# A decay multiply shared by read-out and update, a gate affine folded into activations, and late conditioning blocks spread over three tiles

## The chip, the cores and the metric

The kernel runs on all 8 cores of one Trainium2 chip. Each core computes its own share of the batch; no core waits for another. The metric is the time on the device, in microseconds (us), of the slowest of the eight cores.

Executions of one kernel mostly agree within 0.3%. Some fall into a slower state, more than 1.5% above the fastest run. Ratios here compare fast runs with fast runs; medians take in all runs.

## The reference, cut to what matters

One layer of a decoder trunk: a conditioned normalisation, one input projection, a recurrence over chunks of 64 tokens, a short convolution, an output projection, and then a squared-ReLU MLP. One core has 8 prompt tiles of 256 tokens and one sample tile of 128 tokens.

```python
mod = jax.nn.silu(c) @ w_ada + b_ada                  # conditioning: w_ada is 12 blocks of 512 columns
sh1, sc1, g1, sh2, sc2, g2 = jnp.split(mod[:, None, :], N_MOD, axis=-1)
h = rms_norm(x) * (1 + sc1) + sh1                     # needs blocks 0 to 3
q, fz, i, g, gb, gc, hv = jnp.split(h @ w_in, SPLITS, axis=-1)
logf = jnp.log(lb_h + (1.0 - lb_h) * jax.nn.sigmoid(fz32))      # the gate
k = (1.0 - lb_h) * jax.nn.sigmoid(-fz32)
...
def step(s, inp):                                     # the recurrence over chunks
    d, u = inp
    return d[..., None] * s + u, s                    # the read-out uses s as well
...
x = x + g1 * mix                                      # needs blocks 4 and 5
h2 = rms_norm(x) * (1 + sc2) + sh2                    # needs blocks 6 to 9: "late"
x = x + g2 * (jnp.square(jax.nn.relu(h2 @ w_up)) @ w_down)      # needs blocks 10 and 11: "late"
```

## The kernel before: the parts that matter

A Python list scheduler fixes the order of instructions on each engine when the program is built, from a cost model. At run time each engine goes through its list in that order and waits on semaphores. It knows dependences by buffer *name*, and by overlap of address ranges. A name that covers too much gives a false dependence; a shared address gives a real one.

Weights are fp32 in memory and bf16 on the core; this kernel loads them by casting DMAs that GpSimd issues, at most six under way at a time: each waits for the sixth before it in the program's order. The same GpSimd queue does element-wise work, such as adding the mixer's result to the rows of x.

Loop over tiles, with the loads placed by hand (`n_` counts tiles from 0; tile 3 is the sample tile):

```python
    for n_ in range(2, len(tiles)):
        t0op = len(P.ops)
        if n_ + 1 < len(tiles):
            hs[n_ + 1] = norm1(*tiles[n_ + 1])
        for step in gen(n_):
            if step == "B" and n_ + 1 == len(tiles):
                WB = View(wall[2:6])
                for j in UPORD[:7]:
                    load_up(j)
                norm2(bgroups[0])
        mark = [o for o in P.ops[t0op:] if o.eng == "pe"][20:21]
        if n_ == 4:                                   # four late conditioning blocks behind one tile
            for i, j in enumerate((6, 7, 8, 9)):
                load_ada(j)
                mod_block(j, i % 2 == 0, 24 + 8 * (i // 2), 16 + 8 * (i // 2))
        if n_ == 5:
            load_ada(10); load_ada(11)
            gates(1)
        if 5 <= n_ and conv_i < 4:                    # w_down blocks, fp32 to bf16, memory to memory
            convert(CONV[conv_i], mark)
            conv_i += 1
        if n_ == 6:
            load_dn(0); load_dn(1)
```

Buffers that play a part, and who shares them:

```python
    adaR = Ring("ada", 2, [128, 8, 512], BF16, offset=u0)              # two conditioning blocks
    SbF = (one("rout", [128, 512], F32, offset=u0 + 16384), "rout")    # the last state, to be stored
    ...  # wdn[2], the third w_down block, is placed at u0 + 16384 too
    xrR = Ring("xr", 3, [128, 1024])                                   # rows of x, and the gates' tile
    mix_slot(2, at["p"])
    gfin_b = one("gfin_b", [128, 1024])                                # overlaps the third mix buffer
    modT = one("modT", [128, 32, 17])                                  # all conditioning values, one name
```

A conditioning block ends in a write of `modT`; every normalisation reads `modT`, so a late block's write and the next tile's `hT` are ordered, though they touch different columns:

```python
        tt("dve", modT[:, out_j0:out_j0 + 8, :], ..., ALU.add, [bn, "vecT"], ["modT"])          # in mod_block
        ts("dve", h[:, jj, :], Mb[...], modT[:, 8 + jj, 0:1], modT[:, jj, 0:1], ..., [Mn, "modT"], [hn])   # in norm1
```

The gate, and the recurrence for one chunk:

```python
            act(A_[:], A_[:], AF.Exp, [an], [an], scale=-1.0)
            for i, hd in enumerate(heads):
                ts("dve", F_[...], A_[...], oml[:, hd:hd + 1], lbv[:, hd:hd + 1], ALU.mult, ALU.add, ...)
            act(A_[:], F_[:], AF.Ln, [fn_], [an])
            ...
                        Sb, sbn = SbR.take()
                        tt("pool", v3(Sb), v3(Tp), bdec(dp, cp), ALU.mult, [tpn, dpn], [sbn])   # for the read-out
                        inter(ci, Sb, sbn)
                        for hd in range(4):                                                     # for the update
                            stt(Tn_[...], Tp[...], dp[:, hd, cp:cp + 1], U[...], ALU.mult, ALU.subtract, ...)
```

Of the kernel before, what the change touches and what calls it, by code (L numbers as in the profile page):

```python
# [297 lines left out]
def build_program():  # L298
# [171 lines left out]
        mix.append(t)  # L470

    mix_slot(0); mix_slot(1)
    TsR = Ring("Ts", 2, [128, 512])
    SbR = Ring("Sb", 2, [128, 512], BF16)
    smR = Ring("sm", 2, [128, 512], BF16)
    sqR = Ring("sq", 2, [128, 512], BF16)
# [1 line left out]
    ucar = one("ucar", [128, 4, 32]); uco = one("uco", [128, 4, 32])  # L478
    ucR = Ring("uc", 2, [128, 4, 2])
    decR = Ring("dec", 2, [128, 4, 4]); decS = Ring("decs", 1, [128, 4, 16])  # L480
    lbv = one("lbv", [128, 4]); oml = one("oml", [128, 4])
    vecT = one("vecT", [128, 72]); scT = one("scT", [128, 8, 17], BF16)
    at["p"] = max(at["p"], a0 + 7 * 8192)
    ada0R = Ring("adaf", 4, [128, 8, 512], BF16, offset=k0)
# [106 lines left out]
    tr([(Mb[:, j * 32:j * 32 + 17], ctb[0:17, j * 128:(j + 1) * 128], cB[0:17, 0:17]) for j in range(8)], [ctb_n, "cB"], [Mn])  # L591
    copy("act", scT[:], Mb[:, 0:256].rearrange("p (a b) -> p a b", b=32)[:, :, 0:17], [Mn], ["scT"])
    tt("dve", lbv[:], lbT[:, 1, :], lbT[:, 0, :], ALU.subtract, ["vecT"], ["lbv"])
    act(lbv[:], lbv[:], AF.Exp, ["lbv"], ["lbv"])
    act(lbv[:], lbv[:], AF.Ln, ["lbv"], ["lbv"], bias=1.0)
    act(lbv[:], lbv[:], AF.Exp, ["lbv"], ["lbv"], scale=-1.0)
    ts("dve", oml[:], lbv[:], -1.0, 1.0, ALU.mult, ALU.add, ["lbv"], ["oml"])
    ts("dve", gon, gon, math.sqrt(128.0), None, ALU.mult, None, ["vecT"], ["vecT"])

# [102 lines left out]
    def mixer_tile(kind, ti, last, h, hn, xblk):  # L702
# [12 lines left out]

        for g, heads in enumerate(groups):
            bank, bn = proj(h, hn, 1, heads, TT)
            A_, an = ER.take(); F_, fn_ = WF.take(); C_, cn = WF.take()
            act(A_[:], bank[:, :], AF.Exp, [bn], [an], scale=-1.0)
            act(A_[:], A_[:], AF.Ln, [an], [an], bias=1.0)  # L720
            act(A_[:], A_[:], AF.Exp, [an], [an], scale=-1.0)
            for i, hd in enumerate(heads):
                ts("dve", F_[:, i * TT:(i + 1) * TT], A_[:, i * TT:(i + 1) * TT], oml[:, hd:hd + 1], lbv[:, hd:hd + 1], ALU.mult, ALU.add,
                   [an, "oml", "lbv"], [fn_], mode=1.0)
            act(A_[:], F_[:], AF.Ln, [fn_], [an])
            scan(C_[:], smask, A_[:], ["cBm", an], [cn])
            act(A_[:], C_[:], AF.Exp, [cn], [an])
            act(C_[:], C_[:], AF.Exp, [cn], [cn], scale=-1.0)
            k_, kn = nkR.take()
            stt(k_[:], F_[:], 1.0, C_[:], ALU.subtract, ALU.mult, [fn_, cn], [kn])  # L730
            nk[g] = (k_, kn)
            Eg[g] = (A_, an)
            ev = A_[:].rearrange("p (h c t) -> p h c t", h=NH, t=C)
            copy("pool", dec[:, heads[0]:heads[0] + NH, 0:NCH], ev[:, :, :, C - 1], [an], [dec_n])
        yield "F"

        vt = []
# [43 lines left out]
        for b in range(NB):  # L781
            t0 = b * 128
            v_, vn = vt[b]
            M, Mn = MR.take()
            Mb = M[:, :].bitcast(BF16)
            tr([(Mb[:, hd * 128:(hd + 1) * 128], hv(nk, hd, t0, t0 + 128), ident) for hd in range(4)], dn(nk) + ["cB"], [Mn])
            k_, kn = ktR.take()
            copy("act", k_[:], Mb[:, 0:512], [Mn], [kn])
            M, Mn = MR.take()
            mm([(M[:, hd * 128:(hd + 1) * 128], hv(nk, hd, t0, t0 + 128), hv(qd, hd, t0, t0 + 128), True, True) for hd in range(4)],  # L790
               dn(nk) + dn(qd), [Mn])
            sm, smn = smR.take()
            tt("dve", sm[:].rearrange("p (h t) -> p h t", t=128), M[:, :].rearrange("p (h t) -> p h t", t=128),
               nmask.unsqueeze(1).to_broadcast([128, 4, 128]), ALU.mult, [Mn, "cBm"], [smn])
            O, On = OR.take()
            mm([(O[:, hd * 128:(hd + 1) * 128], v_[:, hd * 128:(hd + 1) * 128], sm[:, hd * 128:(hd + 1) * 128], hd == 0, False) for hd in range(4)],
               [vn, smn], [On])

            def inter(ci, sb, sbn):
                mm([(O[:, hd * 128 + ci * C:hd * 128 + (ci + 1) * C], sb[:, hd * 128:(hd + 1) * 128],  # L800
                     hv(qd, hd, t0 + ci * C, t0 + (ci + 1) * C), False, ci == NCB - 1) for hd in range(4)], [sbn] + dn(qd), [On])

            def bdec(dt_, c):
                return dt_[:, :, c:c + 1].to_broadcast([128, 4, 128])

            v3 = lambda t: t[:].rearrange("p (h v) -> p h v", v=128)
            if kind == "p":
                for ci in range(NCB):
                    c = b * NCB + ci
                    U, Un = UR.take()  # L810
                    mm([(U[:, hd * 128:(hd + 1) * 128], k_[64 * ci:64 * ci + 64, hd * 128:(hd + 1) * 128],
                         v_[64 * ci:64 * ci + 64, hd * 128:(hd + 1) * 128], True, True) for hd in range(4)], [kn, vn], [Un])
                    Tn_, tnn = TsR.take()
                    if state["T"] is None:
                        ts("dve", Tn_[:], U[:, :], -1.0, None, ALU.mult, None, [Un], [tnn], mode=1.0)
                    else:
                        Tp, tpn, dp, dpn, cp = state["T"]
                        Sb, sbn = SbR.take()
                        tt("pool", v3(Sb), v3(Tp), bdec(dp, cp), ALU.mult, [tpn, dpn], [sbn])
                        inter(ci, Sb, sbn)  # L820
                        for hd in range(4):
                            stt(Tn_[:, hd * 128:(hd + 1) * 128], Tp[:, hd * 128:(hd + 1) * 128], dp[:, hd, cp:cp + 1],
                                U[:, hd * 128:(hd + 1) * 128], ALU.mult, ALU.subtract, [tpn, dpn, Un], [tnn])
                    state["T"] = (Tn_, tnn, dec, dec_n, c)
            else:
                for ci in range(NCB):
                    S, Sn = SlR.take()
                    dma("sp", S[:], srec_d[ci], [], [Sn], 262144)
                    Sb, sbn = SbR.take()
                    copy("act", Sb[:], S[:], [Sn], [sbn])  # L830
                    inter(ci, Sb, sbn)
                    km, kmn = kmR.take()
                    ts("dve", km[:], k_[:], cF[:, CR8 + ci:CR8 + ci + 1], None, ALU.mult, None, [kn, "cF"], [kmn], mode=1.0)
                    U, Un = UR.take()
                    mm([(U[:, hd * 128:(hd + 1) * 128], km[:, hd * 128:(hd + 1) * 128], v_[:, hd * 128:(hd + 1) * 128], True, True)
                        for hd in range(4)], [kmn, vn], [Un])
                    tt("dve", S[:], S[:], U[:, :], ALU.subtract, [Sn, Un], [Sn])
                    tt("pool", v3(S), v3(S), bdec(dec, ci), ALU.mult, [Sn, dec_n], [Sn])
                    dma("sp", recs_d[ci], S[:], [Sn], ["recs%d" % ci], 262144)


            sq, sqn = sqR.take()
            act(sq[:], O[:, :], AF.Square, [On], [sqn])
            M, Mn = MR.take()
            mm([(M[:, :], onesb, sq[:], True, True)], [sqn, "cB"], [Mn])
            R_, rn = WT.take()
            act(R_[:], M[:, :], AF.Ln, [Mn], [rn], bias=128.0 * EPS)
            act(R_[:], R_[:], AF.Exp, [rn], [rn], scale=-0.5)
            tt("dve", R_[:], O[:, :], R_[:], ALU.mult, [On, rn], [rn])
            for g, heads in enumerate(groups):  # L850
                h0 = heads[0]
                tt("pool", mx[:, h0:h0 + NH, t0:t0 + 128], R_[:, h0 * 128:(h0 + NH) * 128].rearrange("p (h t) -> p h t", t=128),
                   sg[g][0][:].rearrange("p (h t) -> p h t", t=TT)[:, :, t0:t0 + 128], ALU.mult, [rn, sg[g][1]], [mxn[hd] for hd in heads])
# [191 lines left out]
# [8 lines that stand above are left out]
                    load_up(j)  # L1053
                norm2(bgroups[0])
        mark = [o for o in P.ops[t0op:] if o.eng == "pe"][20:21]
        if n_ == 4:
            for i, j in enumerate((6, 7, 8, 9)):
                load_ada(j)
                mod_block(j, i % 2 == 0, 24 + 8 * (i // 2), 16 + 8 * (i // 2))
        if n_ == 5:  # L1060
            load_ada(10); load_ada(11)
            gates(1)
        if 5 <= n_ and conv_i < 4:
            convert(CONV[conv_i], mark)
            conv_i += 1
        if n_ == 6:
            load_dn(0); load_dn(1)
    load_up(7)
    load_gates(1)
    dma("sp", gfin_b[:], gfin_d.partition_broadcast(128), [], ["gfin_b"], 128 * 4096)  # L1070
# [67 lines left out]
```

## Time and profile before

984.65 us (median of 3 runs, 983.99 to 1009.44). The profiled core has a span of 985.7 us.

| stretch | what runs | what is seen |
|---|---|---|
| 0 to 301 us | loading, tiles 0 to 4, projections of tile 5 | mixed |
| 301 to 357 us | late conditioning blocks 6 to 9 | TensorE busy 23.7 of 56 us |
| 357 to 496 us | last three tiles (6 to 8), about 37 us each, and the last recurrence | TensorE mostly busy |
| 496 to 538.6 us | MLP, first group, up stage | TensorE busy |
| 538.6 us to the end | MLP from the first use of w_down | TensorE busy, DMA share 0.17 from 546 us on |

First the windows view of the kernel before. After the window and its length come the busy times of TensorE, its weight loads, VectorE, ScalarE and GpSimd, each with its number of instructions; then TensorE's granted clock, the share of time that the 16 DMA engines were busy, and GB/s.

```profile
301.00:326.00 25.00, 14.93 (x128) 7.35 (x127) 12.14 (x25) 4.91 (x9) 9.73 (x14) 0.73 0.37 85
326.00:357.00 31.00, 8.80 (x131) 6.09 (x128) 9.07 (x27) 5.17 (x12) 8.14 (x11) 0.57 0.95 148
0.00:301.00 301.00, 210.65 (x1940) 156.42 (x1940) 164.16 (x326) 126.61 (x249) 79.33 (x118) 0.96 0.62 145
301.00:397.00 96.00, 63.72 (x558) 41.31 (x556) 48.27 (x103) 29.96 (x61) 31.55 (x40) 0.77 0.74 146
397.00:538.60 141.60, 126.62 (x964) 84.68 (x963) 91.43 (x186) 61.99 (x126) 46.16 (x58) 0.95 0.90 170
```

In the second line TensorE is busy 8.8 of 31 us.

The chain of waits of the kernel before (start, length, what):

```profile
327.60 21.52 DMA ada_111<-w_ada
...
349.25 1.02 PE U L333 x32
```

TensorE's timeline, then VectorE's, of the kernel before (start, length, instruction; in brackets the idle time before it and what ended it):

```profile
339.21 1.00 PE L333 MATMUL U<-scT,ada_110 128*128 128x17 bf16 x32 [2.66 <-DMA ada_110<-w_ada]
349.25 1.00 PE L333 MATMUL U<-scT,ada_111 128*128 128x17 bf16 x32 [9.04 <-DMA ada_111<-w_ada]
```

```profile
350.36 0.30 DVE L367 TENSOR_TENSOR modT<-U,vecT 128x136 f32<-128x136 f32 x1 [14.54 <-PE U L333]
...
351.11 0.93 DVE L373 TENSOR_SCALAR hT_61<-M,modT 128x256 bf16<-128x256 bf16 x2
```

Blocks 8 and 9 can load only when 6 and 7 have left the two buffers, and the second of them takes 21.5 us to land. The next tile's `hT_61`, whose first transposes were done at 250 us, comes right after the `modT` write: the projections that could fill the gap wait on a name.

GpSimd's timeline of the kernel before, near the MLP's start:

```profile
531.34 0.57 POOL L394 DMA_DIRECT2D wdn_128<-w_down  x1 [32.70 <-DMA recp<-rout]
```

This is a w_down load that waits 32.7 us for the store of the last state, because it will overwrite that state's address. Nothing urgent stands behind it, so the wait is free.

Two groups of the recurrence in the kernel before (busy time, mean ns), of several alike:

```profile
L367 POOL TENSOR_TENSOR Sb_86<-Ts_84,dec_99 128x512 bf16<-128x512 f32 x8 | 8.7, 1085 | 12.4 <-DVE Ts_84 L377 12.4
L377 DVE SCALAR_TENSOR_TENSOR Ts_85<-Ts_84,dec_99,U 128x128 f32<-128x128 f32 x32 | 11.0, 344 | 3.6 <-DVE Ts_84 L377 1.8
```

### The profile page before, as it was taken

How to read it: one execution, taken by the hardware profiler on the slowest of the kernel's cores; microseconds unless marked ns; L12 is line 12 of the kernel's file. 1: busy time of each engine (PE TensorE's matmuls, PEld its weight loads, DVE VectorE, ACT ScalarE, POOL GpSimd, SP SyncE). 2: the span in 40 equal slices, each digit the busy share in tenths (PEclk: the TensorE clock that was granted, in tenths of full speed). 3: DMA queues.
4: the chain of work that ended last, by engine and by line, in shares of the span. 5: the costliest groups of instructions: out<-in, count | busy, mean ns of one | idle time of the engine just before them, and what ended most of it. 6: DMA issues, size and time to landing. Idle time of an engine off the chain costs nothing.

```text
span 985.7 us, 16852 instructions; the slowest of 8 cores (974.9 to 985.7 us)
## 1 busy us (share of the span) xinstructions
PE 836.5 (85%) x5929; PEld 519.7 (53%) x5929; DVE 477.4 (48%) x948; ACT 336.8 (34%) x711; POOL 202.1 (21%) x249
## 2 busy tenths in 40 slices
PE   0168888788775469999599999999999999999995
PEld 0147755466553247677355456545545654654762
DVE  1156566487735256966844334614443451451321
ACT  3056362256522044644334123313312330421321
POOL 1000134442234324345320110010021012001101
PEclk9999999799987769999799999999999999999998
DMA  8999760427133797859999821131022002101101
GB/s 162 206 189 186 163 181 23 150 100 226 68 92 87 145 169 171 172 144 167 172 192 180 258 88 68 45 107 43 22 86 86 1 23 85 44 2 43 64 2 43
DMA packets 27245, 109.75 MB, mean 111 GB/s; under 512 B 3781, under 2 KB 4165, under 8 KB 22298
## 3 DMA queue, kind: packets, MB, share of 16 engines
q0 software_dynamic: 5232, 39.19, 24.7%
q1 hardware_dynamic: 17034, 51.65, 16.3%
q10 hardware_dynamic: 4896, 17.83, 5.9%
q8 instruction: 48, 0.79, 0.3%
q14 instruction: 35, 0.29, 0.1%
HBM read 125.36 MB, written 26.69 MB: 154 GB/s over the span
## 4 chain that ended last, share of the span: by engine, by line
PE 64%; DMA 12%; DVE 10%; issue 7%; ACT 4%; POOL 1%; DVEq 0%; ACTq 0%; POOLq 0%
PE G L333 34%; PE U L333 21%; PE O L333 8%; DMA win_44<-w_in 4%; DMA ada_111<-w_ada 2%; DMA xn_145<-xp 2%; DMA xn_145<-x 2%; DVE Ts_84 L377 1%; PE M L344 1%; DMA cB<-constB 1%; DVE Ts_85 L377 1%; ACT W_140 L360 1%; DVE h2T L373 1%; DVE W_137 L367 1%; DVE W_142 L377 1%
## 5 line engine op out<-in xcount | busy, mean ns | idle before, releaser
L373 DVE TENSOR_SCALAR h2T<-M,modT 128x128 bf16<-128x128 bf16 x128 | 43.9, 343 | 25.4 <-PE M L344 15.4
L360 ACT ACTIVATE W_135<-xn_145 128x1024 bf16<-128x1024 f32 x17 | 17.9, 1052 | 60.6 <-PE M L344 35.3
L344 PE MATMUL M<-cB,W_134 128*128 128x128 bf16 (+1 forms) x144 | 13.6, 234 | 25.7 <-DVE W_134 L367 17.2
L360 ACT ACTIVATE W_134<-xn_144 128x1024 bf16<-128x1024 f32 x17 | 17.9, 1053 | 49.8 <-PE M L344 40.0
L367 POOL TENSOR_TENSOR xr_146<-xr_146,W_137 128x512 f32<-128x512 f32 x9 | 12.1, 1346 | 94.0 <-DVE W_137 L367 93.5
L360 ACT ACTIVATE W_139<-G 128x384 f32<-128x384 f32 (+2 forms) x29 | 14.4, 496 | 42.2 <-PE G L333 41.3
L344 PEld LDWEIGHTS M<-cB,W_134 128*128 128x128 bf16 (+1 forms) x144 | 10.5, 107 | 28.0 <-issue 26.5
L367 DVE TENSOR_TENSOR uT<-W_137,G 128x384 bf16<-128x384 f32 (+1 forms) x26 | 13.7, 528 | 20.9 <-ACT W_137 L360 20.2
L367 POOL TENSOR_TENSOR xr_146<-xr_146,W_136 128x512 f32<-128x512 f32 x5 | 6.6, 1325 | 83.8 <-DVE W_136 L367 83.8
L367 POOL TENSOR_TENSOR xr_146<-xr_146,W_138 128x512 f32<-128x512 f32 x7 | 9.2, 1311 | 62.4 <-DVE W_138 L367 62.2
L344 PE MATMUL M<-cB,W_135 128*128 128x128 bf16 x136 | 13.4, 239 | 9.7 <-DVE h2T L373 5.6
L333 PE MATMUL G<-wdn_127,uT 128*128 128x512 bf16 x88 | 20.8, 379 | 0.0
L333 PE MATMUL G<-wdn_129,uT 128*128 128x512 bf16 x88 | 20.8, 379 | 0.0
L333 PE MATMUL G<-wdn_126,uT 128*128 128x512 bf16 x88 | 20.8, 379 | 0.0
L333 PE MATMUL G<-wdn_128,uT 128*128 128x512 bf16 x88 | 20.8, 379 | 0.0
L367 DVE TENSOR_TENSOR uT<-W_136,G 128x384 bf16<-128x384 f32 (+1 forms) x24 | 12.9, 538 | 16.0 <-ACT W_136 L360 14.5
L367 DVE TENSOR_TENSOR W_137<-U,Gp 128x512 f32<-128x512 f32 x17 | 11.7, 687 | 18.2 <-PE U L333 18.2
L360 ACT ACTIVATE W_136<-G 128x384 f32<-128x384 f32 (+1 forms) x24 | 11.4, 474 | 25.9 <-PE G L333 25.9
L333 PE MATMUL G<-hT_60,win_44 128*128 128x256 bf16 (+1 forms) x128 | 16.8, 300 | 3.6 <-DMA win_44<-w_in 3.5
L367 DVE TENSOR_TENSOR modT<-U,vecT 128x136 f32<-128x136 f32 x4 | 1.2, 300 | 38.3 <-PE U L333 38.3
L367 DVE TENSOR_TENSOR uT<-W_138,G 128x384 bf16<-128x384 f32 (+1 forms) x24 | 13.0, 542 | 13.8 <-ACT W_138 L360 13.8
L333 PE MATMUL G<-hT_61,win_44 128*128 128x256 bf16 x128 | 17.5, 290 | 2.3 <-DVE hT_61 L373 1.4
(566 smaller groups left out, 2191.8 us busy)
## 6 DMA issues: line engine op xcount, KB each, us to landing
xn_145<-x ACTq DMA_DIRECT2D x9, 512.0 KB, 3.6
xn_144<-xp ACTq DMA_DIRECT2D x8, 512.0 KB, 10.6
xn_145<-xp ACTq DMA_DIRECT2D x8, 512.0 KB, 12.8
ada_110<-w_ada POOLq DMA_DIRECT2D x4, 1024.0 KB, 20.2
ada_111<-w_ada POOLq DMA_DIRECT2D x4, 1024.0 KB, 23.1
wscr<-w_down POOLq DMA_DIRECT2D x4, 1024.0 KB, 22.7
xn_144<-x ACTq DMA_DIRECT2D x8, 512.0 KB, 3.8
xr_147<-xp SPq DMA_DIRECT2D x6, 512.0 KB, 11.2
```

Source lines behind the costliest of these rows:

```text
L333: ins = e.matmul(o_, lhsT=l_, rhs=r_, start=st, stop=sp_, skip_group_check=True)
L344: ins = e.transpose(out=o_, in_=i_, identity=id_)
L360: return P.op("act", lambda e: e.activation(out=out, in_=in_, func=func, **kw), r, w, c, prio=prio)
L367: return P.op(eng, lambda e: e.tensor_tensor(out=out, in0=in0, in1=in1, op=op), r, w, vec_cost(eng, out, mode), prio=prio)
L373: f = lambda e: e.tensor_scalar(out=out, in0=in0, scalar1=s1, scalar2=s2, op0=op0, op1=op1)
L377: return P.op("dve", lambda e: e.scalar_tensor_tensor(out=out, in0=in0, scalar=scalar, in1=in1, op0=op0, op1=op1), r, w, vec_cost("dve", o ...
```

## The change

It has three parts. **Decay**: the decayed state is computed once on VectorE, copied to bf16 by ScalarE for the read-out, and used by the update; GpSimd is relieved of it. **Gate**: the affine map goes into the scale and bias operands of ScalarE's Ln, a factor into Exp's bias, and a VectorE operation goes away. **Spread**: late blocks 6 to 11 are loaded two per tile, one tile ahead of their use; the gates and the first two w_down loads move to tile 7.

```diff
-    TsR = Ring("Ts", 2, [128, 512])
+    TsR = Ring("Ts", 1, [128, 512]); SdR = Ring("Sd", 1, [128, 512])
...
-                ts("dve", F_[:, i * TT:(i + 1) * TT], A_[:, i * TT:(i + 1) * TT], oml[:, hd:hd + 1], lbv[:, hd:hd + 1], ALU.mult, ALU.add,
-                   [an, "oml", "lbv"], [fn_], mode=1.0)
-            act(A_[:], F_[:], AF.Ln, [fn_], [an])
-            scan(C_[:], smask, A_[:], ["cBm", an], [cn])
-            act(A_[:], C_[:], AF.Exp, [cn], [an])
-            act(C_[:], C_[:], AF.Exp, [cn], [cn], scale=-1.0)
+                act(L_[:, i * TT:(i + 1) * TT], A_[:, i * TT:(i + 1) * TT], AF.Ln, [an, "oml", "lbv"], [ln_],
+                    scale=oml[:, hd:hd + 1], bias=lbv[:, hd:hd + 1])
+            scan(C_[:], smask, L_[:], ["cBm", ln_], [cn])
+            act(L_[:], C_[:], AF.Exp, [cn], [ln_])
+            for i, hd in enumerate(heads):
+                act(C_[:, i * TT:(i + 1) * TT], C_[:, i * TT:(i + 1) * TT], AF.Exp, [cn, "lnoml"], [cn], scale=-1.0, bias=lnoml[:, hd:hd + 1])
...
+                        S_, ssn = SdR.take()
+                        tt("dve", v3(S_), v3(Tp), bdec(dp, cp), ALU.mult, [tpn, dpn], [ssn])
                         Sb, sbn = SbR.take()
-                        tt("pool", v3(Sb), v3(Tp), bdec(dp, cp), ALU.mult, [tpn, dpn], [sbn])
+                        copy("act", Sb[:], S_[:], [ssn], [sbn])
                         inter(ci, Sb, sbn)
-                        for hd in range(4):
-                            stt(Tn_[:, hd * 128:(hd + 1) * 128], Tp[:, hd * 128:(hd + 1) * 128], dp[:, hd, cp:cp + 1],
-                                U[:, hd * 128:(hd + 1) * 128], ALU.mult, ALU.subtract, [tpn, dpn, Un], [tnn])
+                        tt("dve", Tn_[:], S_[:], U[:, :], ALU.subtract, [ssn, Un], [tnn])
...
-        if n_ == 4:
-            for i, j in enumerate((6, 7, 8, 9)):
-                load_ada(j)
-                mod_block(j, i % 2 == 0, 24 + 8 * (i // 2), 16 + 8 * (i // 2))
-        if n_ == 5:
-            load_ada(10); load_ada(11)
+        if n_ in (5, 6):
+            for i in range(2):
+                mod_block(4 + 2 * (n_ - 4) + i, i == 0, 24 + 8 * (n_ - 5), 16 + 8 * (n_ - 5))
+        if n_ == 7:
             gates(1)
+            load_dn(0); load_dn(1)
+        if n_ in (4, 5, 6):
+            load_ada(6 + 2 * (n_ - 4)); load_ada(7 + 2 * (n_ - 4))
         if 5 <= n_ and conv_i < 4:
             convert(CONV[conv_i], mark)
             conv_i += 1
-        if n_ == 6:
-            load_dn(0); load_dn(1)
```

More of the change, by code (lines that the diff above doesn't have):

```diff
@@ L480, in build_program @@
     decR = Ring("dec", 2, [128, 4, 4]); decS = Ring("decs", 1, [128, 4, 16])
-    lbv = one("lbv", [128, 4]); oml = one("oml", [128, 4])
+    lbv = one("lbv", [128, 4]); oml = one("oml", [128, 4]); lnoml = one("lnoml", [128, 4])
     vecT = one("vecT", [128, 72]); scT = one("scT", [128, 8, 17], BF16)
@@ L593, in build_program @@
     tt("dve", lbv[:], lbT[:, 1, :], lbT[:, 0, :], ALU.subtract, ["vecT"], ["lbv"])
-    act(lbv[:], lbv[:], AF.Exp, ["lbv"], ["lbv"])
-    act(lbv[:], lbv[:], AF.Ln, ["lbv"], ["lbv"], bias=1.0)
-    act(lbv[:], lbv[:], AF.Exp, ["lbv"], ["lbv"], scale=-1.0)
+    act(oml[:], lbv[:], AF.Exp, ["lbv"], ["oml"])
+    act(oml[:], oml[:], AF.Ln, ["oml"], ["oml"], bias=1.0)
+    tt("dve", lnoml[:], lbv[:], oml[:], ALU.subtract, ["lbv", "oml"], ["lnoml"])
+    act(lbv[:], oml[:], AF.Exp, ["oml"], ["lbv"], scale=-1.0)
     ts("dve", oml[:], lbv[:], -1.0, 1.0, ALU.mult, ALU.add, ["lbv"], ["oml"])
@@ L717, in mixer_tile @@
             bank, bn = proj(h, hn, 1, heads, TT)
-            A_, an = ER.take(); F_, fn_ = WF.take(); C_, cn = WF.take()
+            A_, an = WF.take(); L_, ln_ = ER.take(); C_, cn = WF.take()
             act(A_[:], bank[:, :], AF.Exp, [bn], [an], scale=-1.0)
@@ L722, in mixer_tile @@
             for i, hd in enumerate(heads):
-                ts("dve", F_[:, i * TT:(i + 1) * TT], A_[:, i * TT:(i + 1) * TT], oml[:, hd:hd + 1], lbv[:, hd:hd + 1], ALU.mult, ALU.add,
-                   [an, "oml", "lbv"], [fn_], mode=1.0)
-            act(A_[:], F_[:], AF.Ln, [fn_], [an])
-            scan(C_[:], smask, A_[:], ["cBm", an], [cn])
-            act(A_[:], C_[:], AF.Exp, [cn], [an])
-            act(C_[:], C_[:], AF.Exp, [cn], [cn], scale=-1.0)
+                act(L_[:, i * TT:(i + 1) * TT], A_[:, i * TT:(i + 1) * TT], AF.Ln, [an, "oml", "lbv"], [ln_],
[4 more added lines that the diff above has]
+                act(C_[:, i * TT:(i + 1) * TT], C_[:, i * TT:(i + 1) * TT], AF.Exp, [cn, "lnoml"], [cn], scale=-1.0, bias=lnoml[:, hd:hd + 1])
             k_, kn = nkR.take()
-            stt(k_[:], F_[:], 1.0, C_[:], ALU.subtract, ALU.mult, [fn_, cn], [kn])
+            stt(k_[:], A_[:], 1.0, C_[:], ALU.subtract, ALU.mult, [an, cn], [kn])
             nk[g] = (k_, kn)
-            Eg[g] = (A_, an)
-            ev = A_[:].rearrange("p (h c t) -> p h c t", h=NH, t=C)
-            copy("pool", dec[:, heads[0]:heads[0] + NH, 0:NCH], ev[:, :, :, C - 1], [an], [dec_n])
+            Eg[g] = (L_, ln_)
+            ev = L_[:].rearrange("p (h c t) -> p h c t", h=NH, t=C)
+            copy("pool", dec[:, heads[0]:heads[0] + NH, 0:NCH], ev[:, :, :, C - 1], [ln_], [dec_n])
         yield "F"
```

## The prediction

> **What bounds the kernel now.** Busy time by window shows two regimes. From 546 us to the end TensorE is busy 428 of 430 us at clock 1.00: the MLP, which the diff does not touch. Before it lies the mixer. In steady state a prompt tile takes 37 us (the last input projection ends at 397, 435 and 472 us in TensorE's timeline), TensorE 94% busy. From 301 to 357 us that breaks down: busy 14.9 of 25 us, then 8.8 of 31 us, at clocks 0.73 and 0.57.
>
> **Why.** The chain of waits has a 21.5 us piece there, the load of ada_111: four late conditioning blocks (6 to 9) run behind one tile on two buffers, so 8 and 9 load only after 6 and 7 are consumed (issued at 327 us, used at 339 and 349). The stall spreads, because the program tracks modT as one buffer: VectorE's hT_61 multiplies, whose transposes were done at 250 us, directly follow the modT write at 350.8 us. So the next tile's projections, which would fill the recurrence's gaps from about 305 us on, start at 357. The work in 301 to 397 is about 52 us at full rate (projections 24, two output projections 14, recurrences 6, conditioning 7, transposes 2); with steady-state overhead and 5 us of latency 60 us, against 96: 36 us lost.
>
> **Change 1, blocks spread.** Two per tile, each loaded a tile ahead: removes that stall and the false wait, about 36 us, all critical. About 5 us of conditioning work only moves.
>
> **Give-back.** DMA is 0.8 busy from 357 to 472 us and saturated from 472 to 546. The same bytes must pass in less time, and two w_down loads (6.5 us each of all 16 engines, from the queue's 24.7% for 37 MB) move next to the w_up loads, which landed only 10 to 12 us before use. I expect 4 to 8 us back around the MLP's start.
>
> **Change 2, decay.** Per chunk VectorE does two operations of 0.69 us (128x512 tensor_tensor rows) in place of four of 0.34, issued 0.45 apart: 0.3 us less. GpSimd loses 31 x 1.07 us, ScalarE gains 31 x 0.62. From state to bf16 state, 1.05 us on GpSimd becomes 0.69 + 0.62 on two engines: neutral, with a small risk, as ScalarE is in-order and half busy. The Trainium skill ("VectorE: DVE Perf Modes") has fp32 tensor_tensor at one element per cycle; 0.69 us for 512 agrees.
>
> **Change 3, gate.** Per group VectorE loses 2 x 0.53 us; one Ln and one Exp become two halves each with per-partition operands. The skill ("ScalarE: Activation LUTs", What ACT_TABLE_LOAD costs) gives 93 ns per such operand; here a 128x256 one takes 0.51 us with one, 0.38 without. ScalarE gains about 0.75 us per group, 13 in all, off the critical path (20 of 37 us busy per tile); the chain is 0.5 us shorter. Changes 2 and 3 together: 0 to 8 us, before 300 us and in the last recurrence (472 to 487).
>
> **Sum.** 985 - 36 + 6 - 3 = 952 us, 8 in 10 between 937 and 970. Faster by over 2%: 0.87; within: 0.11; slower: 0.02.
>
> **What would show it.** No conditioning load from 300 us on in the chain; clock near 1.0 in 300 to 360 us; hT_61 right after its transposes; the MLP starting near 463 us and taking as long as before; GpSimd 33 us less busy, ScalarE 33 more, VectorE 18 less.
>
> **What would make it wrong.** DMA saturation at the MLP's start returning over 10 us; modT writes now holding up the seventh and eighth tile's hT; ScalarE delaying the bf16 state; a different static instruction order costing elsewhere.

## More of the kernel before

After its mixer a tile adds the output projection to its rows of x and stores them for the MLP:

```python
            xr, xrn = xrR.take()
            dma("sp", xr[:], src, [], [xrn], 128 * 4096)
            for dh in range(2):
                ...
                tt("dve", W[:], bank[:, :], G[:, sl], ALU.mult, [bn, gn], [Wn])
                tt("pool", xr[:, sl], xr[:, sl], W[:], ALU.add, [xrn, Wn], [xrn])
            dma("sp", x1_d[xblk + b], xr[:], [xrn], ["x1_%d" % (xblk + b)], 128 * 4096)
```

## The result, and the profile after

The changed kernel took 990.42 us (median of 4 runs, 989.2 to 1048.7) against 985.22 us (4 runs, 983.99 to 1009.44) for the kernel before in the same rounds. The ratio is 1.0053, 95% interval 1.003 to 1.0076: half a per cent slower, within 2%. Ratios here are the mean time of one kernel's fast runs over that of the other's fast runs of the same rounds, so they are not quite the ratio of the medians quoted.

| us on the profiled core | before | after | difference |
|---|---|---|---|
| MLP starts (first up matmul) | 495.9 | 465.8 | 30.1 sooner |
| w_down first used | 538.6 | 539.4 | 0.8 later |
| first group's up stage, the difference of the two | 42.7 | 73.6 | 30.9 longer |
| last instruction (span) | 985.7 | 987.6 | 1.9 later |

The mixer gained 30 us, as intended. The first up stage gave all of it back. The windows of the kernel after:

```profile
301.00:326.00 25.00, 23.48 (x189) 15.22 (x187) 19.05 (x28) 15.74 (x31) 9.52 (x13) 1.00 0.26 68
326.00:357.00 31.00, 26.56 (x253) 17.88 (x251) 16.86 (x31) 11.13 (x21) 9.06 (x13) 0.89 0.65 135
0.00:301.00 301.00, 213.01 (x1962) 158.93 (x1963) 164.44 (x290) 147.61 (x299) 66.94 (x105) 0.95 0.64 150
301.00:397.00 96.00, 83.20 (x755) 56.38 (x753) 60.90 (x103) 50.54 (x101) 30.57 (x40) 0.93 0.58 129
397.00:539.40 142.40, 108.65 (x746) 67.81 (x744) 70.12 (x125) 50.97 (x109) 27.81 (x39) 0.88 1.01 186
```

TensorE is busy 50 of the 56 us from 301 to 357, against 23.7; its clock is 1.00 and 0.89 there. The Trainium skill ("TensorE: Matmul & The Clock Gate", What's actually happening) says that an idle array falls to half its clock; the 0.57 in the stall before, a mean over idle and busy parts, and the recovery here agree with it. But the DMA share went the other way, from 0.37 and 0.95 down to 0.26 and 0.65. From 397 us to the first use of w_down it went from 0.90 up to 1.01.

Multiply each share by its window. Before the first use of w_down the DMA engines worked 0.62 x 301 + 0.74 x 96 + 0.90 x 141.6 = 385 us in the kernel before, and 0.64 x 301 + 0.58 x 96 + 1.01 x 142.4 = 392 us after (the shares are rounded, so each sum is good to some 3 us). It is nearly the same amount of work, done by nearly the same moment. By 397 us the changed kernel had done *less* of it, 248 us against 258. The stall in 326 to 357 had been idle time for TensorE but working time for the DMA. One caution: all DMA work that came before the first use is counted here, needed for it or not. The four conversions, for example, serve w_down blocks 4 to 7; the kernel before first reads block 4 at 561.1 us, 22.5 us after the first use of w_down.

TensorE's timeline of the kernel after: the new waits, inside the MLP's first up stage.

```profile
480.60 2.72 PE L333 MATMUL U<-h2T,wup_54 128*128 128x384 bf16 x8 [9.43 <-DVE W_137 L367]
490.21 4.38 PE L333 MATMUL G<-h2T,wup_54 128*128 128x384 bf16 x16 [5.54 <-DVE uT L367]
518.32 1.11 PE L333 MATMUL U<-h2T,wup_57 128*128 128x384 bf16 x3 [9.64 <-DMA wup_57<-w_up]
```

Its chain of waits there, in order of time:

```profile
429.89 17.94 DMA x<-xr_149
...
447.89 38.13 DMA xr_149<-xp
...
486.17 1.26 POOL xr_149 L367
...
488.76 29.42 DMA wup_57<-w_up
...
518.32 2.71 PE U L333 x8
```

A row block of x is stored (17.9 us), its buffer is filled with the last tile's rows (38.1 us), GpSimd adds the projection to them, and only then issues the last w_up load, which takes 29.4 us to land. GpSimd's timeline of the kernel after shows why the addition holds up the loads:

```profile
441.83 0.55 POOL L394 DMA_DIRECT2D wup_58<-w_up  x1
...
446.94 0.59 POOL L394 DMA_DIRECT2D wup_56<-w_up  x1
...
455.34 0.72 POOL L394 DMA_DIRECT2D wup_55<-w_up  x1
478.41 1.25 POOL L367 TENSOR_TENSOR xr_148<-xr_148,W_137 128x512 f32<-128x512 f32 x1 [22.34 <-DMA xr_148<-xp]
...
481.01 0.57 POOL L394 DMA_DIRECT2D wup_59<-w_up  x1
486.17 1.25 POOL L367 TENSOR_TENSOR xr_149<-xr_149,W_139 128x512 f32<-128x512 f32 x1 [4.59 <-DMA xr_149<-xp]
...
488.76 0.57 POOL L394 DMA_DIRECT2D wup_57<-w_up  x1
```

GpSimd works through its list in order: it stood 22.3 us at an addition whose rows had not come, with two w_up loads behind it. The order of the list matters too. TensorE first uses `wup_57` ahead of `wup_56` and `wup_59`, but here it is issued last of the eight; in the kernel before it was issued at 464.4 us, ahead of `wup_58` (468.9), `wup_56` and `wup_59`. Its load has to wait for the sixth GpSimd load before it, which is the second w_down load, and the change has moved that load next to it. So of the three waits above the first two (9.4 and 5.5 us) are for rows, through buffers that the late additions still have to read, and the third (9.6 us) is for a block that the new order puts last. The Trainium skill ("DMA: Bandwidth & Descriptors", Issuing engines are not separate DMA queues) says that transfers run on the same 16 engines and interleave whoever issues them. That agrees: the rows are issued by SyncE and the weights by GpSimd, and the rows took 38.1 us between the weights. The same page (Anatomy of one DMA) fits about 2.0 us plus the bytes over 436 GB/s for one transfer on GpSimd's path; an estimate from it for 512 KB is 3.2 us (the rows are SyncE's, so it is a yardstick only). In the kernel before, nine 512 KB row loads for the MLP (`xn_145<-x`) took 3.6 us in the median; most of them are issued in the quiet part, when the MLP runs. In the saturated stretch it is ten times that.

The recurrence and the gate, groups of the kernel after:

```profile
L367 DVE TENSOR_TENSOR Ts_84<-Sd_85,U 128x512 f32<-128x512 f32 x31 | 21.1, 680 | 0.6
L367 DVE TENSOR_TENSOR Sd_85<-Ts_84,dec_98 128x512 f32<-128x512 f32 x16 | 12.2, 765 | 1.1 <-ACT Sb_86 L360 0.4
L360 ACT ACTIVATE Sb_86<-Sd_85 128x512 bf16<-128x512 f32 x16 | 10.0, 628 | 52.0 <-DVE Sd_85 L367 51.9
L360 ACT ACTIVATE WX_116<-W_142,lbv,oml 128x256 f32<-128x256 f32 x12 | 7.1, 595 | 0.1
L360 ACT ACTIVATE W_143<-W_143,lnoml 128x256 f32<-128x256 f32 x16 | 8.0, 502 | 0.7 <-ACT st_162 L360 0.3
```

GpSimd's busy time fell from 202.1 to 170.1 us, ScalarE's rose from 336.8 to 366.1, VectorE's fell from 477.4 to 468.2. The Trainium skill ("ScalarE: Activation LUTs", What ACT_TABLE_LOAD costs) gives 93 ns for each per-partition operand. The trace agrees: 595 ns with two, 502 with one, and 380 to 384 with none for the same 128x256.

### The profile page after: what moved, and what is told of

The parts are those of the page before. It is cut to its first block, busy times and chain, and to the rows that moved or that the text cites. A ratio compares the mean times of both kernels' runs of the same rounds, so it can differ in the third digit from the quotient of the medians.

```text
span 987.6 us, 16715 instructions; the slowest of 8 cores (979.0 to 987.6 us)
## 1 busy us (share of the span) xinstructions
PE 840.5 (85%) x5929; PEld 520.3 (53%) x5929; DVE 468.2 (47%) x851; ACT 366.1 (37%) x780; POOL 170.1 (17%) x218
## 3 DMA queue, kind: packets, MB, share of 16 engines
q0 software_dynamic: 5232, 39.19, 24.8%
q1 hardware_dynamic: 17034, 51.65, 16.1%
## 4 chain that ended last, share of the span: by engine, by line
PE 62%; DMA 16%; DVE 9%; issue 6%; ACT 5%; POOL 1%; ACTq 0%; DVEq 0%; POOLq 0%; SPq 0%
PE G L333 32%; PE U L333 20%; PE O L333 8%; DMA win_44<-w_in 4%; DMA xr_149<-xp 4%; DMA wup_57<-w_up 3%; DMA xn_146<-xp 2%; DMA x<-xr_149 2%; PE M L344 1%; DMA cB<-constB 1%; DVE Sd_85 L367 1%; DVE h2T L373 1%; ACT W_140 L360 1%; ACT W_142 L360 1%; PE M L333 1%
## 5 line engine op out<-in xcount | busy, mean ns | idle before, releaser
L360 ACT ACTIVATE W_140<-G 128x384 f32<-128x384 f32 (+2 forms) x38 | 19.7, 519 | 57.9 <-PE G L333 57.5
L344 PE MATMUL M<-cB,W_135 128*128 128x128 bf16 (+1 forms) x144 | 13.8, 235 | 25.9 <-DVE W_135 L367 16.3
L360 ACT ACTIVATE W_135<-xn_145 128x1024 bf16<-128x1024 f32 x17 | 17.9, 1053 | 43.1 <-PE M L344 41.5
L360 ACT ACTIVATE Sb_86<-Sd_85 128x512 bf16<-128x512 f32 x16 | 10.0, 628 | 52.0 <-DVE Sd_85 L367 51.9
L367 POOL TENSOR_TENSOR xr_147<-xr_147,W_138 128x512 f32<-128x512 f32 x8 | 10.4, 1296 | 94.8 <-DVE h2T L373 49.2
L360 ACT ACTIVATE W_136<-xn_146 128x1024 bf16<-128x1024 f32 x17 | 17.8, 1049 | 23.6 <-PE M L344 17.9
L367 DVE TENSOR_TENSOR uT<-W_137,G 128x384 bf16<-128x384 f32 (+1 forms) x24 | 12.9, 537 | 24.9 <-ACT W_137 L360 23.5
L367 POOL TENSOR_TENSOR xr_147<-xr_147,W_137 128x512 f32<-128x512 f32 x5 | 6.6, 1329 | 97.1 <-DVE W_137 L367 97.1
L333 PE MATMUL G<-h2T,wup_54 128*128 128x384 bf16 (+1 forms) x96 | 17.8, 343 | 5.5 <-DVE uT L367 5.5
L367 DVE TENSOR_TENSOR Ts_84<-Sd_85,U 128x512 f32<-128x512 f32 x31 | 21.1, 680 | 0.6
L367 DVE TENSOR_TENSOR W_138<-U,Gp 128x512 f32<-128x512 f32 x17 | 11.7, 689 | 20.2 <-PE U L333 20.2
L367 DVE TENSOR_TENSOR W_137<-U,Gp 128x512 f32<-128x512 f32 x13 | 8.9, 688 | 25.9 <-POOL xr_148 L367 14.1
L360 ACT ACTIVATE W_140<-W_140 128x512 f32<-128x512 f32 x32 | 20.1, 628 | 2.1
L367 DVE TENSOR_TENSOR uT<-W_138,G 128x384 bf16<-128x384 f32 (+1 forms) x26 | 13.7, 528 | 13.9 <-ACT W_138 L360 13.2
L360 ACT ACTIVATE W_139<-xr_147 128x1024 bf16<-128x1024 f32 x2 | 2.1, 1057 | 48.8 <-POOL xr_147 L367 48.8
## 6 DMA issues: line engine op xcount, KB each, us to landing
xr_148<-xp SPq DMA_DIRECT2D x6, 512.0 KB, 15.8
```

What stands on the lines that cost most here:

```text
L333: ins = e.matmul(o_, lhsT=l_, rhs=r_, start=st, stop=sp_, skip_group_check=True)
L344: ins = e.transpose(out=o_, in_=i_, identity=id_)
L360: return P.op("act", lambda e: e.activation(out=out, in_=in_, func=func, **kw), r, w, c, prio=prio)
L367: return P.op(eng, lambda e: e.tensor_tensor(out=out, in0=in0, in1=in1, op=op), r, w, vec_cost(eng, out, mode), prio=prio)
```

## The experiments

**Theory.** Before w_down can be used, a nearly fixed amount of DMA work has to be done. The spread removed TensorE's wait but left the DMA its work, and moved some of it later. Rows of x and w_up loads then come late in a saturated DMA. **Rivals.** (a) The decay and gate parts cost time, through ScalarE or the changed order. (b) The gates hold one of three buffers for rows of x (`xrR`) from 393 us until their store, issued at 434 us, and that alone delays the last tile's rows. (c) The two w_down loads, now next to the w_up loads, do the damage. (d) The static order of GpSimd's list, not the volume.

All kernels gave correct results. The kernel before ran along, with medians 987.72 (e1 to e4), 984.87 (e5 to e8) and 985.36 us (e9 to e12). The medians below take in slow runs (one of e1's four, two of e2's five, one of e7's four); the ratios do not.

| label | what | median us | ratio to before | 95% interval |
|---|---|---|---|---|
| e1 | decay and gate, old conditioning | 1012.00 | 1.0250 | 1.0219 to 1.0281 |
| e2 | spread alone | 1000.06 | 1.0106 | 1.0068 to 1.0143 |
| e3 | after, gates in another buffer | 990.41 | 1.0036 | 1.0017 to 1.0056 |
| e4 | after, w_down loads last | 992.83 | 1.0064 | 1.0047 to 1.0082 |
| e5 | after, conversions three tiles earlier | 969.36 | 0.9841 | 0.9825 to 0.9858 |
| e6 | after, spread one tile earlier | 1000.67 | 1.0161 | 1.0145 to 1.0177 |
| e7 | e1, last state in another buffer | 985.38 | 1.0001 | 0.9984 to 1.0018 |
| e8 | e5, e6 and e7's buffer together | 971.15 | 0.9868 | 0.9847 to 0.9889 |
| e9 | e5 and e7's buffer | 971.84 | 0.9856 | 0.9830 to 0.9882 |
| e10 | e9 without decay and gate | 975.14 | 0.9888 | 0.9858 to 0.9918 |
| e11 | before, conversions earlier | 993.85 | 1.0082 | 1.0057 to 1.0107 |
| e12 | e8, late conditioning values under their own name | 963.22 | 0.9775 | 0.9749 to 0.9801 |

### The parts alone: e1, e2, and e7

e1 takes the spread out of the kernel after; e2 puts only the spread into the kernel before.

```diff
 # e1, from after (e2 is the reverse, from before)
-        if n_ in (5, 6): ...
-        if n_ == 7:
-            gates(1)
-            load_dn(0); load_dn(1)
-        if n_ in (4, 5, 6): ...
+        if n_ == 4: ...
+        if n_ == 5:
+            load_ada(10); load_ada(11)
+            gates(1)
+        if n_ == 6:
+            load_dn(0); load_dn(1)
```

> The changed kernel with the conditioning blocks put back behind one tile (decay and gate changes only). Theory 'late loads': the spread alone causes both the gain of about 30 us up to the start of the MLP and the loss of about 34 us in its first group, and decay and gate are worth little: 978 to 986 us, the 20 us stall near 330 to 350 us is back, the MLP's first group runs without waits for x rows or w_up. Rival 'decay and gate cost': the spread gained and the new ScalarE work took it back: over 1005 us.

> The kernel before with only the conditioning blocks spread. Late loads: 985 to 996 us, with the MLP started near 466 us and again some 30 us of waits in its first group (x rows of the last tile landing near 480 us). Decay and gate cost: about 955 us.

Both missed, e2 by little (fast runs 995.08, 995.54 and 1000.06 us, the last one profiled). e2 shows the same picture as the kernel after: the MLP starts at 484.7 us (before: 495.9), has two waits of 8.5 and 7.9 us in its first up stage, and uses w_down first at 550.7. So the give-back belongs to the spread. But its MLP starts 18.9 us later than the kernel after's. Up to 397 us TensorE had worked alike (82.7 and 83.2 us busy from 301 us on, before: 63.7); then a load of rows for the MLP (`xn<-x`, 22.1 us from 408.2 us) stands in e2's chain, ScalarE waits 9.9 us for it with the tile's gate behind it in its list, and TensorE stands 9.9 us.

e1 was the surprise, at 1012.0 us. It has nothing new in the DMA, yet TensorE stood 21.8 us in the up stage. GpSimd's timeline and the chain of waits of e1 (traces of experiments have no buffer numbers):

```profile
525.70 0.56 POOL L394 DMA_DIRECT2D wdn<-w_down  x1 [25.59 <-DMA recp<-rout]
526.27 1.27 POOL L367 TENSOR_TENSOR xr<-xr,W 128x512 f32<-128x512 f32 x1
```

```profile
483.04 42.13 DMA recp<-rout
```

This is the wait on the store of the last state that was free in the kernel before. The scheduler has now put the last addition to x *behind* the w_down load that waits for the store; the store of 256 KB took 42.1 us in the full DMA (share 1.02 from 483 to 525 us), and the MLP waited for that addition. e7 tests it: the last state goes to the `Sd` buffer, which no load overwrites.

```diff
-            y, yn = SbF
+            y, yn = SdR.take()
```

> Decay and gate changes without the spread, as in e1, but the last state is written to the decay buffer in place of the buffer that the third w_down block overwrites. Theory 'order accident': e1 lost its 21 us because GpSimd's queue waited 25.6 us for the store of that state before it could start a w_down load, with an x addition behind it in the same queue; with the wait gone 982 to 992 us. Rival 'decay and gate cost': still over 1003.

985.38 us, ratio 1.0001. The 25 us of e1, which by its time alone looked like rival (a), were this order accident, and decay plus gate are worth nothing measurable beside the old conditioning: rival (a) falls.

### The buffer and the w_down loads: e3 and e4

```diff
 # e3, from after
-        gt, gt_n = xrR.take()
+        gt, gt_n = xrR.take() if g == 0 else (gfin_b, "gfin_b")
 # e4, from after
-            load_dn(0); load_dn(1)
...
-    for j in range(2, 8):
+    for j in range(8):
         load_dn(j)
```

> The changed kernel, the second gate's bias and result in the buffer of the final gain (free until then) in place of one of the three x-row buffers. Theory 'slot': gates(1), moved two tiles later, holds one of three x-row buffers from 393 to 449 us, so the last tile's x rows are asked for only after the tile before has been stored and queue behind the weight loads; with the slot free the first block's rows are issued near 393 us and land before 440, the 9 us wait near 471 us goes, and the time falls by 8 to 20 us. Rival 'bytes': the DMA engines are saturated from 400 us on and have the same bytes to move, so some other transfer is late in its place: within 4 us of the changed kernel (986 to 994).

> The changed kernel, the first two w_down blocks loaded after the last w_up block in place of before most of them. Theory 'w_down in front': two transfers of 6.5 us of all engines stand in front of w_up and of the x rows; without them the rows land some 13 us earlier, w_up_57 too, and the time falls by 8 to 15 us. Bytes: no gain, the wait moves to the first w_down use (near 550 us). Slot: 0 to 6 us, as the rows are still asked for late.

e3 was a bad test. `gfin_b` shares its address with the third mix buffer, so the mixer had to wait for the gates' store. VectorE's timeline of e3:

```profile
471.24 0.69 DVE L367 TENSOR_TENSOR mix<-G,W 128x512 bf16<-128x512 f32 x1 [20.70 <-DMA gates<-gfin_b]
```

One 20.7 us wait took the place of another, and the time stayed at 990.4. Rival (b) is not settled by it.

e4 speaks against (c) as the whole cause. Without the two w_down loads ahead of it, the last tile's row load still took 39.0 us in the chain and two waits of 9.7 and 6.0 us stayed in the up stage. A new wait of 8.8 us for w_down itself appeared at 547.0 us. Taking bytes out of one place in the stretch put them into another of the same stretch. e4 is also the nearest thing to a test of (d), though it moves the w_down loads as well: by its scheduler, the w_up loads stand in their order of use, and the 9.6 us wait for a w_up block is gone. Yet the time is no better: 992.83 us.

### Fewer bytes in the stretch: e5, e6, e8

e5 changes one line of the kernel after: it converts four w_down blocks during tiles 2 to 5 instead of 5 to 8. The total work is the same; some of it moves to where the DMA was not full. The scheduler then also orders GpSimd's list anew.

```diff
-        if 5 <= n_ and conv_i < 4:
+        if 2 <= n_ and conv_i < 4:
```

> The changed kernel, the four conversions of w_down (a transfer from DRAM to DRAM, which needs no SBUF) started in tiles 3 to 6 of the order in place of 6 to 9. Nothing else moves. Theory 'bytes': what returned the gain is that the DMA engines must move everything up to the first w_down use by about 540 us and run at 1.0 from 400 us on, while they are half idle from 160 to 350; four conversions of about 6.5 us leave the full stretch, so the x rows and w_up land sooner and the first MLP group ends 15 to 26 us sooner: 964 to 976 us. Rival 'slot' (x rows asked for too late because gates(1) holds a buffer): they are still asked for at 440 and 448 us, gain below 8 us.

As expected: 969.36 us, and the give-back shrank. The windows and the chain of e5:

```profile
0.00:301.00 301.00, 212.50 (x1935) 157.89 (x1935) 161.12 (x283) 144.72 (x293) 67.98 (x106) 0.94 0.68 154
301.00:397.00 96.00, 81.83 (x725) 55.17 (x726) 61.06 (x102) 49.13 (x96) 30.41 (x41) 0.93 0.59 132
397.00:521.90 124.90, 109.07 (x801) 70.87 (x799) 73.06 (x132) 56.29 (x119) 26.61 (x37) 0.93 1.00 195
```

```profile
451.91 28.03 DMA xr<-xp
```

The MLP starts at 469.8 us, no sooner than after the change, but w_down is first used at 521.9 instead of 539.4, since the DMA had 13 us more behind it at 397 us. The row load took 28.0 us in place of 38.1, so the rows landed 6 us sooner although they were asked for 4 us later. This is the theory's strongest support, but it is not bytes alone. Running the scheduler of each run's kernel.py gives the order of the w_up blocks after the two w_down loads: 6, 4, 3, 7, 5 after the change, with block 5 (`wup_57`) behind all four additions to the last tile's rows, and 3, 4, 5, 6, 7 in e5, with block 5 ahead of them. So the third wait of the kernel after, 9.6 us, could go with the order, the two for rows with the bytes. e4 had the better order without the early conversions and gained nothing; how the 21 us of e5 divide is not shown.

e6 moves the spread one tile earlier (blocks 6 and 7 used at the end of tile 4, gates and w_down at tile 6), and e8 joins e5, e6 and e7.

```diff
 # e6, from after
+        if n_ == 4:
+            load_ada(6); load_ada(7)
-        if n_ in (5, 6):
+        if n_ in (4, 5):
             for i in range(2):
-                mod_block(4 + 2 * (n_ - 4) + i, i == 0, 24 + 8 * (n_ - 5), 16 + 8 * (n_ - 5))
+                mod_block(6 + 2 * (n_ - 4) + i, i == 0, 24 + 8 * (n_ - 4), 16 + 8 * (n_ - 4))
+            load_ada(8 + 2 * (n_ - 4)); load_ada(9 + 2 * (n_ - 4))
-        if n_ == 7:
+        if n_ == 6:
             gates(1)
             load_dn(0); load_dn(1)
-        if n_ in (4, 5, 6): ...
```

> The changed kernel with the spread of the conditioning blocks one tile earlier (blocks 6 and 7 used at the end of the fifth tile, 8 and 9 sixth, 10 and 11 with the gates seventh; w_down 0 and 1 follow). Bytes: four conditioning loads and two w_down loads leave the full stretch after 400 us (about 13 to 26 us of all engines): 960 to 978 us, even though hT of the seventh tile now waits for the first modT write near 325 us, as in the kernel before. Rival 'nothing but order': within 6 us of the changed kernel.

> The changed kernel with the conditioning one tile earlier, the conversions early, and the last state in the decay buffer. Bytes: the mixer's gain of about 30 us is kept: 948 to 964 us, MLP started near 465 us and its first group without waits over 3 us. Rival: the give-back is a fixed latency of the transition, over 975.

e6 missed by 20 us and more. GpSimd's timeline shows e1's accident again, longer:

```profile
509.14 0.57 POOL L394 DMA_DIRECT2D wdn<-w_down  x1 [37.04 <-DMA recp<-rout]
509.73 1.27 POOL L367 TENSOR_TENSOR xr<-xr,W 128x512 f32<-128x512 f32 x1
```

I did not run e6 with the other buffer alone, so for e6 this cause is read from the trace. e8, which has that buffer, has no wait in its up stage. e8 missed for another reason: 971.15 us, since its MLP starts only at 483.7. From 301 to 326 us TensorE was busy 15.1 of 25 us at clock 0.73, very nearly what it was before the change: moved one tile earlier, the `modT` write stands before the next tile's `hT` again.

### What decay and gate are worth beside the spread: e9 and e10

```diff
 # e9, from after: e5 and e7's buffer
 # e10: the same without decay and gate (from before: spread, early conversions, last state in Ts)
-            y, yn = SbF
+            y, yn = TsR.take()
```

> The changed kernel with early conversions (as e5) and the last state in the decay buffer, so that no w_down load waits for its store. If the bytes are what binds, the two w_down loads start about 20 us sooner and little else changes: 958 to 969 us (e5: 969). If GpSimd's wait for the store was what was left of the give-back: below 958.

> The kernel before with the spread, early conversions and the last state in a free state buffer, without the decay and the gate changes: e9 less those two. Theory 'decay and gate are neutral': within 6 us of e9. Rival 'they cost': more than 6 us faster than e9. As the prediction had it (0 to 8 us worth): up to 8 us slower than e9.

971.84 and 975.14 us, side by side on one chip; the intervals overlap. So decay and gate are worth about 3 us here. With late conversions the same pair is e2 and the kernel after: ratios 1.0106 and 1.0053, about 5 us. They were run at other times. e9 missed its range by 3 us. It also shows that e7's buffer brings nothing where the order is lucky (e5: 0.9841, e9: 0.9856).

### Early conversions without the spread: e11

```diff
 # e11, from before
-        if 5 <= n_ and conv_i < 4:
+        if 2 <= n_ and conv_i < 4:
```

> The kernel before with only the conversions early. Theory: its time is lost in the stall from 326 to 357 us (two conditioning loads behind one another), not at the start of the MLP, where it waited 2 us; so 976 to 987 us, and the early conversions are worth something only with the spread. Rival: early conversions are worth about 20 us by themselves: below 970.

A miss: slower by 0.8%. The fourth conversion is issued just ahead of the two critical conditioning loads. GpSimd's timeline and the chain of e11:

```profile
326.34 0.55 POOL L394 DMA_DIRECT2D wscr<-w_down  x1 [0.26 <-issue]
...
328.11 1.12 POOL L394 DMA_DIRECT2D ada<-w_ada  x2
```

```profile
328.68 26.20 DMA ada<-w_ada
```

The critical load takes 26.2 us instead of 21.5, and the MLP starts at 503.1 us. There was no wait in the up stage to save: it took 42.1 us. The conversions and the spread pay together (e5, e10), and neither pays alone (e11, e2).

### A version that beats both: e12

e12 is e8 with its own name for the conditioning values of the second half, so that their writes no longer stand before the mixer's `hT`.

```diff
+        mn = "modT" if out_j0 < 16 else "modT2"
-               badaT[...], ALU.add, [bn, "vecT"], ["modT"])
+               badaT[...], ALU.add, [bn, "vecT"], [mn])
 # and the readers of columns 16 to 31 (norm2 and the sample tile's second half) read "modT2"
```

> e8 with the conditioning values of the second half under a name of their own, so that hT of the seventh tile no longer waits for the first late block's write. Theory: e8 kept its MLP free of waits but started it near 484 us because of that false wait (TensorE busy 15 of 25 us from 301 on); without it the MLP starts near 468 us: 953 to 964 us. If the MLP then waits again for w_up or x rows, bytes bind once more: 964 to 972.

963.22 us, ratio 0.9775. It beats both kernels; against a threshold of 2% the interval, 0.9749 to 0.9801, just touches the edge. Its MLP starts at 454.3 us, 29.4 us sooner than e8's, but the up stage ends only 10.6 us sooner (515.1 against 525.7; eight early w_down matmuls at 508.2 us are left aside) and the time falls by 8 us. The give-back is at work here too: TensorE waits 14.2 us at 476.5 us. So the time met the range expected without waits partly by luck: the MLP started 14 us sooner than expected, and the waits took that back. Two windows of e12, and its chain, which is again rows of x:

```profile
301.00:397.00 96.00, 91.29 (x868) 64.55 (x867) 75.08 (x127) 57.62 (x117) 32.52 (x46) 1.00 0.77 159
397.00:515.10 118.10, 95.47 (x661) 59.66 (x659) 58.17 (x104) 46.93 (x98) 24.58 (x31) 0.88 1.00 203
```

```profile
422.36 33.63 DMA x<-xr
456.06 15.81 DMA xr<-xp
```

In e12 the gates' store is issued at 393.4 us, so they hold no row buffer then; a store of 33.6 us and a load of 15.8 us still follow one another through the ring of three. That weakens rival (b), but does not measure it.

### DMA work done by 397 us, and the first use of w_down

For the kernels with the spread, leaving out those with a wait of another kind (e3, e4, e6), worked out from the shares as above (for e12, "first used" is the end of the up stage):

| | DMA work done by 397 us | DMA share from there to w_down's first use | w_down first used | median us |
|---|---|---|---|---|
| e2 | 243 | 1.01 | 550.7 | 1000.06 |
| after | 248 | 1.01 | 539.4 | 990.42 |
| e10 | 254 | 0.98 | 526.0 | 975.14 |
| e5 | 261 | 1.00 | 521.9 | 969.36 |
| e8 | 263 | 0.93 | 525.7 | 971.15 |
| e9 | 268 | 1.00 | 520.3 | 971.84 |
| e12 | 288 | 1.00 | 515.1 | 963.22 |

Where the DMA is full from 397 us on, the more it has done by then, the sooner w_down is used. The work up to that use is not quite fixed: it comes to between 380 us (e10) and 406 us (e12). e8, not quite full, is the one that steps out of line: its MLP starts late. In the kernels with the old conditioning the DMA is not full there (0.90 before; by the same sum 0.84 in e7 and 0.78 in e11), and TensorE's stall sets the time.

## Why the prediction was wrong, point by point

- **What bounds the kernel: right as far as it went.** The stall at 301 to 357 us, its cause in the two conditioning buffers, and the false wait through `modT` were as said. `hT_61` now comes with its transposes, the projection that reads it starts at 300.4 us, and no conditioning load stands in the chain from 300 us on.
- **The gain, "about 36 us, all critical": nearly right for the mixer.** The MLP starts at 465.8 us ("near 463"), 30.1 us sooner. It was critical only up to the MLP's start. That the number came so near has some luck in it: the spread alone (e2) starts the MLP only 11.2 us sooner, because a wait for rows takes part of the gain already there.
- **The step that failed: "I expect 4 to 8 us back around the MLP's start."** The mechanism was named, the term of the sum was mis-sized: the first up stage became 30.9 us longer (42.7 to 73.6 us). I had read the DMA share as a risk of some contention, not as an amount of work. The profile of before already held an estimate. 385 us of DMA work precede the first use of w_down and 258 of them were done by 397 us. If all of it has to come first, and if the change brings no more DMA work before 397 us, as this one brings none, then even with every engine busy from there on w_down is not used before 397 + (385 - 258) = 524 us. That is 15 us sooner than 538.6, not 33. The estimate uses only numbers of before; it is no strict bound, since not all of that work is needed for the first use. In fact 10 us of the work moved later than 397 us, and nothing was left.
- **"taking as long as before" for the MLP: wrong in its first group**, right from w_down's first use on (447.1 us before, 448.2 after, to the end of the span).
- **Decay and gate, "0 to 8 us": right.** e7 gives 0, e9 against e10 about 3. GpSimd lost 32.0 us ("33") and ScalarE gained 29.3 ("33"). VectorE lost 9.2 us where I said 18. The gate's multiplies did take 17.5 us away. The decay saved nothing: its two operations per chunk came to 44.3 us (the multiply with a broadcast operand took about 0.75 us, not 0.69) against 42.5 us for the four old ones, which I had counted by their spacing of 0.45 us where 0.34 us each is busy time. Operations that were not changed took the rest, most of all the sample tile's `km` products (12.4 us against 7.8). ScalarE delaying the bf16 state was not seen: of the 52.0 us idle before those copies, 51.9 was for VectorE's product.
- **What would make it wrong:** the list had "DMA saturation at the MLP's start returning over 10 us" and "a different static instruction order costing elsewhere". The first is what happened. The second happened as well, on a smaller scale: `wup_57`, issued last, cost a wait of 9.6 us within the 30.9. It happened at full size in two experiments (e1, e6) that are one step from this change. The chance of 0.13 for not being faster was too small for a change whose gain ran towards a saturated DMA.

What stays open: how much of the 30.9 us is due to the order of GpSimd's list rather than to the bytes (no run changes one alone), how much the gates' hold on a row buffer costs by itself (e3 failed to test it), and how much of the remaining wait in e12 comes from the ring of three row buffers rather than from the bytes.

## What to carry to other kernels

Before you remove a stall, look at what every other resource did during it: time that is idle for TensorE may be the time in which the DMA gets its work done. Add up the DMA work that must precede the next stage and what is done of it by the time you save; with a full DMA the difference is an estimate of how soon the next stage can run, and a gain larger than that needs the bytes moved earlier as well. In a statically ordered queue, keep instructions that others wait for away from those that wait on a buffer's store: a wait that is free in one version costs 25 us in the next, so a part that is tried alone and comes out slow is not yet shown to be bad.

## What the Trainium skill lacked or had wrong

- "DMA: Bandwidth & Descriptors", Anatomy of one DMA: the fit for one transfer has no term for a busy DMA. An estimate from it for 512 KB is 3.2 us; a row load of that size took 38.1 us here while the DMA share was 1.01, and a 256 KB store 42.1 us (e1). The page states the interleaving, but no section says how long a small transfer takes behind 1 MB weight loads.
- The same page, Measured (HBM→SBUF, 128 partitions, SWDGE, issued from GpSimd), and SWDGE vs HWDGE vs iDMA: the casting load is named as GpSimd's, its cost is not. Here GpSimd's queue moved 39.19 MB, counted as landed, for 24.7% of 985.7 us, which is 6.2 us per MB; the main hardware queue moved 51.65 MB for 16.3%, which is 3.1 us per MB. A weight load reads two bytes of fp32 for each byte of bf16 that lands, so per MB read the two come out alike.
- No page that I read says what an in-order GpSimd queue costs when it both computes and issues loads. Here a w_down load that waited for a store held up an addition for 25.6 us (e1) and 37.0 us (e6), and additions that waited for rows held up w_up loads for 22.3 us (after).
